# Row sums by kind, residual products spread, one convolution group earlier, in a one-core diffusion layer with 32 experts

## The chip, the cores and the metric

The kernel runs on one core of a Trainium2 chip. The metric is the device time of one execution, in microseconds (us); lower is better. Five engines work side by side, each in the order of its own queue: TensorE (PE, matrix products; its weight loads are shown as PEld), VectorE (DVE), ScalarE (ACT), GpSimd (POOL) and SyncE (SP), whose queue issues nearly all transfers from memory. They wait for one another by semaphores.

## The reference

One layer of a transformer-like block on 256 latent tokens and 256 context tokens of width 1024, in float32:

```
mod = silu(c) @ w_ada + b_ada                      # shift, scale, gate (twice)
u   = (rms_norm(x) * (1 + scale1) + shift1) @ w_in # 2560 columns, the context likewise
mix = [fourier(f) @ w_fourier, attention(q, k, v, context), b * conv3(c * h)] @ w_out
x   = x + gate1 * mix
t   = rms_norm(x) * (1 + scale2) + shift2
group = argmax(t @ w_rg); experts = top2 of (t @ w_re) in that group
y   = sum over the two experts of weight * (silu(t @ w_gate[e]) * (t @ w_up[e])) @ w_down[e]
out = rms_norm(x + gate2 * y) * norm_final
```

There are 32 experts of hidden width 512. All their weights are read, 6 MB an expert.

## The kernel before

**Weights.** All weights come through one list of transfers (`queue`, line 108), 2 MB each, that SP issues in order. Each goes into one of ten slots of 16 KB a partition (`slabs`); `take` claims a slot, `drop` gives it back when its last reader is named, and `pump` (line 123) issues the next transfers as far as slots are free. A transfer whose slot is still being read waits on SP, and all later ones wait behind it. When the prologue is over an eleventh slot is opened (`more`, line 832).

**Prologue.** The input projection, the adaLN rows, attention, the Fourier and convolution groups, the output projection and the routing logits are cut into named steps. `STEPS` (line 61) is the order in which all steps are written out by hand; each engine executes its own instructions in that order. The steps that matter here:

- `hi{n}`, `lo{n}` (lines 491 to 505): ACT rounds a piece of weights to a short form, DVE takes the rest; three buffers `ws` are used in turn, so `hi19` must wait until the products on piece 16 are done. `lo15` and `lo19` are the last readers of whole slots.
- `q0` to `q3` and `c0` to `c3` (`pairs`, line 571, through `project`, line 508): the 24 products each of one quarter of the queries and of the convolution's two factors. `q3` reads piece 15, `c0` piece 16, `c1` piece 17. `qt0` (ACT) and `qt1` (DVE) copy the finished queries.
- `ss1` (line 433, `sum_rows`, line 411): the first gate's values lie in DVE's sums over a partition each; four products with a column of ones add them over the 128 partitions, and four products with one row add the bias. Each of the four pairs writes its own 32 partitions of one PSUM bank. The other uses of `sum_rows` have no bias.
- `cs`, `csa`: four rows turned to columns by two transposes (PE), then added to a bias (DVE, line 439).
- `ch`, `w1`, `po`, `at`, `fo`, `fy`, `fz`, `mf`, `ml`: the Fourier group. `s{u}`, `X{u}`, `E{u}`, `R{u}`, `S{u}`, `t{u}`: scores (PE, line 664), row minimum (DVE, 673 and 675), exponential (ACT), scaling (DVE, ACT), transposes (PE) of the attention.

All PSUM tiles of the prologue come from one pool of eight banks (`bank`, line 255); a new tile takes a bank that an earlier reader has released.

**Routing** (lines 841 to 858). `py` holds the sums of the result in four PSUM banks; six products with the identity first put the residual `xs` there (line 846: for columns 0 to 512 two products of 512 columns, for 512 to 768 and 768 to 1024 two of 256 each). Then DVE runs the steps of `route` for both token tiles (lines 788 to 796, the last writes `msk`), five products (851 to 854, into `pr`) count the tokens ahead of each, and DVE makes the gather matrices from them (`place`, lines 821 to 823, into `fsr`).

**Experts** (line 1067). `gathered` (905) and `placed` (914, 918) fetch the up to 32 tokens of an expert, `hidden` (932) makes the 64 products with gate and up weights and drops one slot after each half, `project_down` (958) the 32 with the down weights. The next expert's gathering goes between. The sums of four experts are added to `py` by `scatter` (924) a group later, the last ones by `group_add` (1094) and `add` (1121). PSUM tiles come from a pool of seven banks (`mbank`, line 837).

Of the kernel before, what the change touches and what calls it, by code (L numbers as in the profile page):

```python
# [62 lines left out]
z1 w1 hi2 U10 H10 lo2 kx0 hi3 L10 rq1 lo3 fc1 k0 fa1 U11 U01 H11 H01 ar2 L11 hi4 L01 lo4 b3 rq2 fg1 Ba3 B3 fc2 k1 hi5 fa2 U02 lo5  # L63
U12 H02 H12 L02 L12 ar3 hi6 lo6 fg2 rq3 a0 a1 a2 fc3 k2 hi7 fa3 a3 U03 U13 lo7 H03 H13 L03 L13 a4 kv fg3 a5 a6 hi8 k3 gb ft hi9 a7
lo8 lo9 v0 hi10 a8 kt0 kt1 lo10 kt2 kt3 a9 a10 v1 a11 hi11 lo11 a12 v2 hi12 a13 lo12 a14 e0 a15 po0 hi13 e1 q0 lo13 e2 v3 hi14 e3
lo14 e4 ssh vt1 e5 hi15 q1 rsh lo15 vt0 vt3 vt2 e6 q2 hi16 e7 lo16 cs ss1 hi17 csa q3 lo17 ch0 qt1 qt0 hi18 ch1 w10 s1 lo18 w11
at0 po1 X1 s0 at1 fo0 X0 E1 fo1 s2 fy0 R1 E0 fz0 c0 c1 mf0 R0 hi19 ml0 S0 lo19 fy1 rs1 fz1 t0 S1 hi20 s3 X2 mf1 c2 z0_ y0_ E2 ml1
lo20 t1 hi21 R2 ss2 X3 z1_ S2 c3 rs2 y1_ E3 lo21 m0t00 e8 cv0 duh t2 R3 hi22 cv1 m1t00 S3 lo22 p0 cw0 m0t11 ph0 z2_ t3 y2_ cm0 pl0
m0t10 z3_ y3_ s4 cl0 cw1 m0t01 m4t11 hi23 s5 X4 cm1 m1t01 m4t00 cl1 E4 p1 X5 dg g3 R4 E5 lo23 e9 ph1 m2t00 S4 m2t11 pl1 m4t10 R5
e10 t4 S5 m4t01 g3a z4_ y4_ t5 hi24 e11 m2t10 z5_ s6 y5_ lo24 m2t01 s7 X6 hi25 m1t11 m1t10 lo25 E6 p2 X7 hi26 m5t01 ph2 m3t11 R6  # L70
# [7 lines left out]
def tile_kernel(ctx: ExitStack, tc: tile.TileContext, x, cx, small_a, small_b, b_g1, b_g2, w_ada, w_in, w_out, w_gu, w_dn, out):  # L78
    nc = tc.nc
    PE, DVE, ACT, POOL, SP = nc.tensor, nc.vector, nc.scalar, nc.gpsimd, nc.sync  # L80
# [8 lines left out]
    def blk(i, n=P):  # L89
        return slice(i * n, (i + 1) * n)  # L90
# [78 lines left out]
    cs = slab_c[:, 0:2048].rearrange("p (t f) -> p t f", t=2)  # L169
# [8 lines left out]
    bq = slab_g[:, 3332:3844]  # L178
# [14 lines left out]
    ones = keep.tile([P, P], F32, name="ones")  # L193
# [61 lines left out]
    def bank(shape=(P, 512), key=None):  # L255
        b = ps.tile(list(shape), F32, name="b", tag="b", bufs=8)
        if key is not None:
            held[key] = b
        return b
# [78 lines left out]
    def tokens(s):  # L338
        return slice(s * SEQ, (s + 1) * SEQ)
# [71 lines left out]
    def sum_rows(key, a, bias=False):  # L411

        pa = bank((P, 256), key)
        for q in range(4):
            if bias:
                r = slice(32 * (q // 2), 32 * (q // 2) + 1)
                PE.matmul(pa[blk(q, 32), :], ones[r, 0:32], bq[r, blk(q % 2, 256)], start=True, stop=False)
            PE.matmul(pa[blk(q, 32), :], ones[:, 0:32], a[:, blk(q, 256)], start=not bias, stop=True)

    def area():  # L420
# [11 lines left out]
    wr = sa[:, CA["wr"]].rearrange("p (j f) -> p j f", j=NJ)  # L432
    lb = keep.tile([P, 40], F32, name="lb")
    step["ss1"] = lambda: sum_rows("ss1", acc[:, 0:D], True)
    step["rs1"] = lambda: ACT.copy(area()["rg1"], held["ss1"])
    step["ssh"] = lambda: sum_rows("ssh", acc[:, D:2 * D])
    step["rsh"] = lambda: ACT.copy(r1, held["ssh"])
    step["cs"] = lambda: columns("cs", r1, 256)
# [370 lines left out]
    def onehot(g, st, *ts):  # L809

        for t in ts or (slice(0, 2),):
            r = rk[:, t, 4 * g:4 * g + 4]
            n = list(st[:, t].shape)
            DVE.tensor_tensor(st[:, t], r[..., None].to_broadcast(n), iota_r[:, None, :].to_broadcast(n) if len(n) == 3 else
                              iota_r[:, None, None, :].to_broadcast(n), OP.is_equal)
        return st
# [3 lines left out]
    def place(t, p):  # L820
        return [lambda: DVE.scalar_tensor_tensor(rk[:, t, :], msk[:, t, :], -OFF, p, op0=OP.mult, op1=OP.add),
                lambda: onehot(0, fsr, t),
                lambda: DVE.tensor_scalar(fsr[:, t], fsr[:, t], rr[:, t:t + 1], None, op0=OP.mult)]
# [13 lines left out]
    def mbank(shape=(P, 512), tag="b"):  # L837
        return pm.tile(list(shape), F32, name="m", tag=tag, bufs={"b": 7, "f": 1}[tag])


    py = {}
    for a, b in ((0, 512), (512, 768), (768, 1024)):
        whole = mbank((P, 2, 256)) if a else None
        for t in range(2):
            py[t, a, b] = whole[:, t, :] if a else mbank()
            PE.matmul(py[t, a, b], ident, xs[:, t, a:b], start=(t == 0 or not a), stop=False)  # L846
    pr = mbank((P, 3, NE))
    for fs in zip(*routes):
        for f in fs:
# [2 lines left out]
    for i, first_ in ((1, trib), (2, onesb)):  # L852
        PE.matmul(pr[:, i, :], onesb, msk[:, 0, :], start=True, stop=False)
        PE.matmul(pr[:, i, :], first_, msk[:, 1, :], start=False, stop=True)
    for fs in zip(place(0, pr[:, 0, :]), place(1, pr[:, 1, :])):
        for f in fs:
            f()
# [21 lines left out]
    def group(g):  # L879

        st = fst if g == 0 else onehot(g, mo.tile([P, 2, 4, CAP], F32, name="st"))
        if g:
            DVE.tensor_tensor(fsr, st, rr[:, :, None, None].to_broadcast([P, 2, 4, CAP]), OP.mult)
        state[g] = [st, None, None]

    def weighted(g):

        sw = mo.tile([P, 2, 4, CAP], F32, name="sw", tag="sw")
        POOL.tensor_tensor(sw, state[g][0], cmb[:, :, 4 * g:4 * g + 4, None].to_broadcast([P, 2, 4, CAP]), OP.mult)
        return sw  # L890

    def turned(g, sw):
        pg = mbank((P, 2, P))
        for t in range(2):
            PE.transpose(pg[:, t, :], sw[:, t], ident)
        state[g][1] = mo.tile([P, 2, P], F32, name="sl", tag="sl")
        ACT.copy(state[g][1], pg)
        return pg

    def gathered(e):  # L900

        pg = mbank((P, 256))
        for t in range(2):
            for q in range(4):
                PE.matmul(pg[32 * q:32 * q + 32, :], fsr[:, t, e % 4, :], xs[:, t, blk(q, 256)], start=(t == 0), stop=(t == 1))  # L905
        gt = mo.tile([P, 256], F32, name="gt", tag="gt")
        (DVE.tensor_copy if e == 0 else ACT.copy)(gt, pg)  # L907
        return gt

    def placed(e, gt):  # L910

        pt = mbank((P, 2, 4, CAP))
        for c in range(2):
            PE.transpose(pt[:, c], gt[:, blk(c)], ident)  # L914
        dst = xg[:, e % 4].rearrange("p (q c) n -> p c q n", c=2)
        for v, op, src in ((a2, OP.mult, pt), (sh2, OP.add, dst)):
            w = v.rearrange("p o (q c) -> p (o c) q", c=2)[..., None].to_broadcast([P, 2, 4, CAP])
            DVE.tensor_tensor(dst, src, w, op)  # L918

    def scatter(g):  # L920

        _, sl, yg = state[g]
        for (t, a, b), p in py.items():
            PE.matmul(p, sl[:, t, :], yg[:, a:b], start=False, stop=False)  # L924
# [28 lines left out]
    def project_down(e, ht, yg, i):  # L953
        wdn = loaded["dn", e].rearrange("p (q k f) -> p q k f", q=4, k=4)
        pd = mbank((P, 256))
        for k in range(4):
            for q in range(4):
                PE.matmul(pd[32 * q:32 * q + 32, :], ht[:, 32 * k:32 * k + 32], wdn[:, q, k, :], start=(k == 0), stop=(k == 3))  # L958
        drop(f"dn_{e}")
        pump()  # L960
        for q in range(4):
            rows = blk(q, 32)
            DVE.tensor_tensor(yg[blk(i, 32), blk(q, 256)], pd[rows, :], g2q[rows, :], OP.mult)  # L963

    def upto(e, also={}):

        got = {}

        def fetch():
            got["gt"] = gathered(e + 1)  # L970

        def put():
            placed(e + 1, got["gt"])

        if e in (15, NE - 1):
            return hidden(e)
        return hidden(e, {NJ: [fetch], NJ + 1: [put]} | also)

    def expert(e, also={}):
        g, i = divmod(e, 4)  # L980
        ht = upto(e, also)
        if i == 2 and g < NE // 4 - 1:
            group(g + 1)
        if i == 0:
            if g not in (0, 4):
                scatter(g - 1)
            state[g][2] = mo.tile([P, D], F32, name="yg", tag="yg")
        if i == 2:
            pg = turned(g, state[g][1])
            if e > NE - 4:  # L990

                for q in range(4):
                    (ACT.copy if q % 2 else DVE.tensor_copy)(sl1[blk(q, 32)], pg[blk(3, 32)])
        project_down(e, ht, state[g][2], i)
        if i == 1:
            state[g][1] = weighted(g)
# [69 lines left out]
    weights()  # L1066
    for e in range(NE - 4):
        expert(e)
        if e == 15:
            scatter(3)  # L1070
            n_over = nc.values_load(over[0:1, 0:1], min_val=0, max_val=1)
            with tc.If(n_over > 0):  # L1072
                overflow()
            xg = tokens()
            placed(e + 1, gathered(e + 1))
# [12 lines left out]
    e = NE - 1  # L1088
# [1 line left out]
    n = 3 * CAP  # L1090

    def group_add(k):
        (t, a, b), p = list(py.items())[k]
        PE.matmul(p, sl[0:n, t, :], yg[0:n, a:b], start=False, stop=False)  # L1094

    for k in range(6):
        group_add(k)
# [6 lines left out]
    py = {(t, a): p for (t, a, b), p in py.items()}  # L1104
# [47 lines left out]
    r = [fs[:, 6, t:t + 1] for t in range(2)]  # L1152
    a, b = 512, 768
# [95 lines left out]
```

## Time and profile before

| | us |
|---|---|
| median of 3 runs | 633.53 |
| lowest and highest | 633.09, 634.85 |
| profiled execution, whole | 633.33 |
| its span, first to last instruction | 631.5 |
| PE busy in it | 486.7 (77%) |
| DVE busy | 248.3 (39%) |
| ACT busy | 127.9 (20%) |

Times in rows are microseconds from the start of the span, unless they are marked ns. The chain of waits starts at the last instruction and goes back, at each step, to what released it; each of its pieces is a time at which nothing else would have made the end come sooner. The timeline shows instructions in order of time, neighbours of one kind merged (x8 is eight of them), with the idle time of the engine before them and who ended it in brackets. The windows give busy time of each engine in a stretch, the granted clock of TensorE (1.00 is 2.4 GHz, 0.50 is 1.2 GHz), and what the 16 DMA engines moved.

### The profile page before, as it was taken

The numbers are of one execution on the slowest core, as the hardware profiler recorded it, in microseconds if no ns is written. First come the engines' busy times: TensorE is split into PE (matmuls) and PEld (weight loads), VectorE is DVE, ScalarE is ACT, GpSimd is POOL, SyncE is SP. The second block draws the span as 40 slices with busy tenths as digits, with TensorE's granted clock in tenths as the row PEclk, the third lists the DMA queues.
The fourth block names the chain that finished last, engine by engine and source line by source line (L and its number), as shares of the span: only waits on it lengthen the run. The fifth ranks groups of instructions, "written<-read, shape, count | busy, mean of one in ns | idle before, by whom it ended". The sixth has DMA issues, their size and how long they took to land.

```text
span 631.5 us, 11826 instructions
## 1 busy us (share of the span) xinstructions
PE 486.7 (77%) x5175; PEld 301.2 (48%) x5175; DVE 248.3 (39%) x589; ACT 127.9 (20%) x281; POOL 10.1 (2%) x20
## 2 busy tenths in 40 slices
PE   3899999999989995775577666866766676568784
PEld 3788886866755553342234323433423342234442
DVE  5949784798563533111211121222132111211124
ACT  4564334765430100000000000000000000001113
POOL 1000000000000000000000000000000000000000
PEclk9899999999999999788979787888888897977998
DMA  8999983389999999999999999999999999999992
GB/s 336 425 422 404 398 342 134 134 323 393 392 398 390 428 428 427 421 428 428 424 425 428 425 425 421 423 427 429 423 425 424 427 428 425 425 425 428 425 364 92
DMA packets 21223, 246.18 MB, mean 390 GB/s; under 512 B 2214, under 2 KB 3242, under 8 KB 6956
## 3 DMA queue, kind: packets, MB, share of 16 engines
q1 hardware_dynamic: 21016, 245.08, 93.4%
q8 instruction: 43, 0.70, 0.5%
q10 hardware_dynamic: 148, 0.27, 0.1%
q14 instruction: 16, 0.13, 0.1%
HBM read 244.28 MB, written 1.05 MB: 388 GB/s over the span
## 4 chain that ended last, share of the span: by engine, by line
DMA 62%; PE 33%; DVE 2%; ACT 1%; issue 1%; DVEq 0%; SPq 0%; ACTq 0%
DMA gu<-in_w_gu 38%; DMA dn<-in_w_dn 24%; PE b L524 13%; PE b L722 4%; PE m L932 3%; PE b L664 1%; PE m L958 1%; PE b L709 1%; PE b L699 1%; PE b L310 1%; PE m L1121 1%; DVE a L293 1%; PE m L905 1%; PE m L846 1%; PE m L1094 1%
## 5 line engine op out<-in xcount | busy, mean ns | idle before, releaser
L932 PE MATMUL m<-gu,xg 128*32 128x256 f32 x2048 | 157.1, 460 | 99.3 <-DMA gu<-in_w_gu 94.3
L932 PEld LDWEIGHTS m<-gu,xg 128*32 128x32 f32 x2048 | 77.0, 127 | 172.4 <-issue 66.8
L942 DVE TENSOR_TENSOR hh<-m,sg 128x128 f32<-128x128 f32 x32 | 9.3, 292 | 221.1 <-ACT sg L940 221.1
L940 ACT ACTIVATE sg<-m 128x128 f32<-128x128 f32 x32 | 8.9, 277 | 338.1 <-PE m L932 338.1
L963 DVE TENSOR_TENSOR yg<-m,g2q 32x256 f32<-32x256 f32 x124 | 52.1, 420 | 59.0 <-PE m L958 57.7
L958 PE MATMUL m<-dn,ht 128*32 128x256 f32 x992 | 61.1, 387 | 8.7 <-DMA dn<-in_w_dn 7.4
L524 PE MATMUL b<-uh,ws 128*128 128x256 f32 (+1 forms) x240 | 52.3, 309 | 0.0
L958 PEld LDWEIGHTS m<-dn,ht 128*32 128x32 f32 x992 | 31.1, 110 | 30.0 <-issue 7.6
L524 PEld LDWEIGHTS b<-uh,ws 128*128 128x128 f32 x240 | 39.5, 190 | 4.8 <-issue 2.8
L905 PE MATMUL m<-xs,fsr 128*32 128x256 f32 x512 | 38.6, 420 | 3.2 <-PEq L1072 2.2
L524 PE MATMUL b<-ul,ws 128*128 128x256 f32 (+1 forms) x120 | 36.3, 306 | 0.0
L524 PE MATMUL b<-ws,uh 128*128 128x512 f32 (+1 forms) x96 | 26.5, 364 | 2.4 <-ACT uh L353 2.4
L500 DVE TENSOR_TENSOR ws<-in,ws 128x1024 fp32r<-128x1024 f32 x20 | 24.4, 1223 | 9.3 <-ACT ws L495 9.2
L905 PEld LDWEIGHTS m<-xs,fsr 128*32 128x32 f32 x512 | 19.0, 125 | 18.7 <-issue 9.7
L924 PE MATMUL m<-yg,sl 128*128 128x256 f32 (+1 forms) x84 | 27.1, 473 | 1.0 <-DVE yg L963 1.0
L495 ACT CAST ws<-in 128x1024 fp32r<-128x1024 f32 x20 | 21.0, 1048 | 32.4 <-PE b L524 30.7
L722 PE MATMUL b<-ws,cat 128*128 128x512 f32 x96 | 27.4, 414 | 0.0
L524 PEld LDWEIGHTS b<-ul,ws 128*128 128x128 f32 x120 | 22.9, 193 | 0.9
L918 DVE TENSOR_TENSOR xg<-m,a 128x256 f32<-128x256 f32 x32 | 13.6, 425 | 21.9 <-PE m L914 21.9
L914 PE MATMUL m<-ident,gt 128*128 128x128 f32 x64 | 14.0, 301 | 9.3 <-ACT gt L907 8.2
L924 PEld LDWEIGHTS m<-yg,sl 128*128 128x128 f32 x84 | 16.1, 198 | 10.7 <-issue 7.8
L722 PEld LDWEIGHTS b<-ws,cat 128*128 128x128 f32 x96 | 16.5, 188 | 7.5 <-issue 4.1
(250 smaller groups left out, 497.6 us busy)
## 6 DMA issues: line engine op xcount, KB each, us to landing
gu<-in_w_gu SPq DMA_DIRECT2D x63, 2048.0 KB, 39.3
dn<-in_w_dn SPq DMA_DIRECT2D x31, 2048.0 KB, 39.2
ada<-in_w_ada SPq DMA_DIRECT2D x12, 2048.0 KB, 12.5
in<-in_w_in SPq DMA_DIRECT2D x3, 2048.0 KB, 9.5
in<-in_w_in SPq DMA_DIRECT2D x8, 512.0 KB, 15.9
out<-in_w_out SPq DMA_DIRECT2D x2, 2048.0 KB, 8.9
gu<-in_w_gu SPq DMA_DIRECT2D x4, 512.0 KB, 28.5
dn<-in_w_dn SPq DMA_DIRECT2D x3, 512.0 KB, 11.5
```

The lines of the kernel that those rows point to most:

```text
L495: ACT.copy(ws[:, 0], loaded[kind, i][:, blk(c, 1024)])
L500: DVE.tensor_tensor(split[n][:, 1], loaded[kind, i][:, blk(c, 1024)], split[n][:, 0].bitcast(F32), OP.subtract)
L524: PE.matmul(po, st, mv, start=begins, stop=(c == 3 and tail and not any(po is v[1] for v in todo[n + 1:])))
L722: PE.matmul(held["yo", t, h], held["cat"][:, a, MIX[n], blk(t)], ws[:, b, h, :], start=(held["nm", t, h] == 0), stop=(held["nm", t, h] == ...
L905: PE.matmul(pg[32 * q:32 * q + 32, :], fsr[:, t, e % 4, :], xs[:, t, blk(q, 256)], start=(t == 0), stop=(t == 1))
L914: PE.transpose(pt[:, c], gt[:, blk(c)], ident)
L918: DVE.tensor_tensor(dst, src, w, op)
L924: PE.matmul(p, sl[:, t, :], yg[:, a:b], start=False, stop=False)
L932: PE.matmul(pg[32 * q:32 * q + 32], xg[:, e % 4, j, :], wgu[j // 4][:, :, j % 4, q * P:(q + 1) * P], start=(j == 0), stop=(j == NJ - 1))
L942: DVE.tensor_tensor(hh, pg[:, 1, :], sg, OP.mult)
L958: PE.matmul(pd[32 * q:32 * q + 32, :], ht[:, 32 * k:32 * k + 32], wdn[:, q, k, :], start=(k == 0), stop=(k == 3))
L963: DVE.tensor_tensor(yg[blk(i, 32), blk(q, 256)], pd[rows, :], g2q[rows, :], OP.mult)
```

## The change

In `sum_rows` the four bias products come first, then the four sums; before they alternated. In `STEPS`, `q3` moves ahead of `cs` and `ss1`, and `c0` moves from before `c1` to after `ch1`, ahead of `s1`. Of the six residual products the two of columns 768 to 1024 stay ahead of the routing, the two of 512 to 768 go behind the five counting products, and the two of 0 to 512 go behind expert 1. `group_add` sorts the pieces so that it takes them in the order it had; `scatter` now takes them in the new order.

```diff
-lo14 e4 ssh vt1 e5 hi15 q1 rsh lo15 vt0 vt3 vt2 e6 q2 hi16 e7 lo16 cs ss1 hi17 csa q3 lo17 ch0 qt1 qt0 hi18 ch1 w10 s1 lo18 w11
-at0 po1 X1 s0 at1 fo0 X0 E1 fo1 s2 fy0 R1 E0 fz0 c0 c1 mf0 R0 hi19 ml0 S0 lo19 fy1 rs1 fz1 t0 S1 hi20 s3 X2 mf1 c2 z0_ y0_ E2 ml1
+lo14 e4 ssh vt1 e5 hi15 q1 rsh lo15 vt0 vt3 vt2 e6 q2 hi16 e7 lo16 q3 cs ss1 hi17 csa lo17 ch0 qt1 qt0 hi18 ch1 c0 w10 s1 lo18 w11
+at0 po1 X1 s0 at1 fo0 X0 E1 fo1 s2 fy0 R1 E0 fz0 c1 mf0 R0 hi19 ml0 S0 lo19 fy1 rs1 fz1 t0 S1 hi20 s3 X2 mf1 c2 z0_ y0_ E2 ml1
...
         pa = bank((P, 256), key)
+        for q in range(4) if bias else ():
+            r = slice(32 * (q // 2), 32 * (q // 2) + 1)
+            PE.matmul(pa[blk(q, 32), :], ones[r, 0:32], bq[r, blk(q % 2, 256)], start=True, stop=False)
         for q in range(4):
-            if bias:
-                r = slice(32 * (q // 2), 32 * (q // 2) + 1)
-                PE.matmul(pa[blk(q, 32), :], ones[r, 0:32], bq[r, blk(q % 2, 256)], start=True, stop=False)
             PE.matmul(pa[blk(q, 32), :], ones[:, 0:32], a[:, blk(q, 256)], start=not bias, stop=True)
...
-    for a, b in ((0, 512), (512, 768), (768, 1024)):
+
+    def residual(a, b):
         whole = mbank((P, 2, 256)) if a else None
         for t in range(2):
             py[t, a, b] = whole[:, t, :] if a else mbank()
             PE.matmul(py[t, a, b], ident, xs[:, t, a:b], start=(t == 0 or not a), stop=False)
+
+    residual(768, 1024)
     pr = mbank((P, 3, NE))
...
+    residual(512, 768)
     for fs in zip(place(0, pr[:, 0, :]), place(1, pr[:, 1, :])):
...
         expert(e)
+        if e == 1:
+            residual(0, 512)
...
-        (t, a, b), p = list(py.items())[k]
+        (t, a, b), p = sorted(py.items(), key=lambda v: (v[0][1], v[0][0]))[k]
```

## Rows read from the trace of the kernel before

**Rows 1.** The page: data rate in 40 slices of 15.8 us each.

```profile
GB/s 336 425 422 404 398 342 134 134 323 393 392 398 390 428 428 427 421 428 428 424 425 428 425 425 421 423 427 429 423 425 424 427 428 425 425 425 428 425 364 92
```

**Rows 2.** The chain of waits in order of time: start, length, engine and line.

```profile
90.46 0.57 PE b L418 x8
...
97.10 0.54 PE b L417 x2
...
100.92 0.55 PE b L418 x2
101.47 3.02 PE b L524 x24
104.49 1.73 PE b L596 x8
106.22 1.06 PE b L664 x4
...
180.93 3.71 PE m L846 x12
...
188.84 5.35 PE m L932 x64
...
197.83 3.45 PE m L932 x64
...
214.17 32.15 DMA dn<-in_w_dn
```

**Rows 3.** Windows: a stretch, then each engine's busy time, TensorE's clock, DMA share, GB/s.

```profile
130.00:165.00 35.00, 35.00 (x232) 22.46 (x233) 28.23 (x70) 20.47 (x39) 0.00 (x0) 1.00 0.99 401
...
192.00:195.00 3.00, 3.00 (x53) 1.87 (x45) 0.29 (x1) 0.28 (x1) 0.00 (x0) 0.93 0.82 246
```

**Rows 4.** SP's waits between 98 and 119 and between 182 and 193; its timeline there.

```profile
SPq L152 <- DVE ws L500: 21.3, 1, 21.3
...
SPq L152 <- PE m L932: 11.3, 1, 11.3
...
117.84 10.13 SPq L152 DMA_DIRECT2D ada<-in_w_ada  x2
...
192.39 0.33 SPq L152 DMA_DIRECT2D dn<-in_w_dn  x1
```

**Rows 5.** Timeline: four products of one row each, in one run.

```profile
187.75 0.63 PE L1063 MATMUL m<-sa,ones 1*32 1x256 f32 x8
```

**Rows 6.** Timeline of DVE and ACT between 84 and 122.

```profile
103.13 0.17 DVE L439 TENSOR_TENSOR sh<-b,sa 128x8 f32<-128x8 f32 x1 [6.61 <-DMA sa<-in_b_g]
...
104.53 0.69 DVE L580 COPY a<-b 128x512 f32<-128x512 f32 x1
...
107.31 0.42 DVE L673 CUSTOM_DVE_ANT_0 acc<-b,a 128x256 f32<-128x256 f32 x1 [0.48 <-PE b L664]
...
109.43 0.42 DVE L673 CUSTOM_DVE_ANT_0 acc<-b,a 128x256 f32<-128x256 f32 x1 [0.29 <-PE b L664]
...
116.58 1.23 DVE L500 TENSOR_TENSOR ws<-in,ws 128x1024 fp32r<-128x1024 f32 x1 [2.21 <-ACT ws L495]
...
115.50 1.05 ACT L495 CAST ws<-in 128x1024 fp32r<-128x1024 f32 x1 [1.89 <-PE b L524]
```

**Rows 7.** Timeline of the routing.

```profile
182.52 0.31 DVE L796 TENSOR_TENSOR msk<-oh 128x32 bf16<-128x32 f32 x2
...
184.47 0.18 PE L851 MATMUL m<-msk,trib 128*128 128x32 bf16 x1
...
184.79 0.28 DVE L821 SCALAR_TENSOR_TENSOR rk<-msk,m 128x32 f32<-128x32 bf16 x2 [1.96 <-PE m L854]
...
185.76 1.07 PE L905 MATMUL m<-xs,fsr 128*32 128x256 f32 x16 [1.00 <-DVE fsr L823]
```

**Rows 8.** Windows over the first expert's products.

```profile
189.50:192.00 2.50, 2.50 (x28) 1.62 (x24) 0.79 (x4) 0.00 (x0) 0.61 (x1) 0.50 1.01 433
...
192.50:193.00 0.50, 0.50 (x16) 0.38 (x12) 0.00 (x0) 0.00 (x0) 0.00 (x0) 1.00 0.74 295
```

## The prediction

> **What bounds the kernel now.** I read the page's data rate first. From the 14th slice on it stands at 421 to 429 GB/s, almost to the end, while the two slices around 95 to 126 us have 134 [rows 1]: so the time is a long stretch in which the transfers never rest, put behind a prologue in which they do. Second, the chain of waits: up to 181 us it is nearly all PE, piece after piece, through the routing and the first experts PE and DVE, and from 214.17 on only transfers that queue behind one another [rows 2]. Third, the windows: PE is busy 35.00 of 35 us in the prologue's second half, DVE 28.23 [rows 3]. Fourth, SP's waits: its longest one, 21.3 us, is for DVE's last reading of a slot (`lo19`), and the last long one, 11.3 us, for the first half of expert 0's products, after which it issues at 192.39 [rows 4]. Around that moment the rate falls to 246 GB/s over 3 us [rows 3]; against 426 that is 540 KB short, or 1.27 us of transfer time. It is the last hole. After it an expert takes PE about 7.2 us (two from 197.83 to 214.17, less half an expert's 3.45 [rows 2]) and gives back three slots, whose filling takes 3 x 4.9 us (2.1 MB at 426 GB/s). PE is then always ahead.
>
> So what counts is when the transfers become unbroken. Two things set that: when the last transfers issued during the prologue run dry (call it D), and when expert 0 gives back its first slot (R, at 192.39). If everything up to 181 comes earlier by p, D moves by p. If the routing gives another r, R moves by p + r. The end moves by p plus the part of the hole that closes, at most 1.27 us.
>
> **Part 1, the row sums.** Today eight products alternate, bias, sum, bias, sum: from 97.10 to 101.47, eight pieces of 0.54 or 0.55, 4.37 us in all [rows 2]. The same four sums without bias take 0.57 when they run together, as at 90.46 [rows 2], since the four write different quarters of the partitions. Four one-row products in one run take 0.63 [rows 5], the nearest row to the bias group. That makes 0.57 + 0.63 = 1.2 us, with 0.1 for the one change between the kinds 1.3; 4.37 - 1.3 = 3.1 us less PE, on the path. The bounds: at best no change of kind costs anything (-3.2); at worst the four bias products don't overlap, four at 0.54 as now, so 2.16 + 0.57 = 2.73 and -1.6. I take 3.1, since [rows 5] is the same form.
>
> One difference speaks against it: the products at 187.75 read four different groups of rows, while the bias products share two, two by two. The Trainium skill (TensorE: Matmul & The Clock Gate, Part 3: Packing small matmuls) says that a weight load overlaps running products only where the row group differs; by that two and two would follow each other. The four sums share all rows and run in 0.57 together [rows 2], so the row says otherwise; by the page the gain would be nearer the 1.6, which is a rival below.
>
> **Part 2, q3 and c0 moved.** Nothing is added: 24 products each, 3.02 us [rows 2], change place on an engine that never idles there. So PE gains nothing by itself, and the question is who now waits. From about 97 PE does q3 (3.02), the columns, the sums (1.3), ch0 and ch1 (1.73), c0 (3.02) and s1 (1.06): s1 ends near 107.2, where it ends now, at 107.28 [rows 2], so the first row minimum still starts near 107.3 [rows 6]. The saved 3.1 us stand in PE's queue as c0 already done. DVE is held till 103.13 by a transfer that doesn't move [rows 6], and after it has the copy `qt1` and two `lo` steps to do; with c0 ahead of s1 PE has work meanwhile. Between 107.3 and 118 DVE must make up 3.1 us. It can: its largest pause there, 2.21 us, is for the cast `hi19`, which waited for c0's products on PE (ACT idle 1.89) [rows 6], and c0 is now long done; smaller pauses add the rest. I expect `lo19`, and with it the transfer that heads SP's queue, 2.5 us before 117.84, between 0 and 3.1; behind it stand the last adaLN and the first expert weights, whose users also come 3 us earlier. I put the lag that reaches PE at 0, bounds 0 to 2.9. So p = 3.1.
>
> **Part 3, the residual products.** Six products of 2048 columns take 3.71 us [rows 2], 0.46 for 256 columns. DVE has `msk` ready at 182.83 (182.52 + 0.31), but the counting products start at 184.47, behind the residual, and DVE goes on at 184.79 after 1.96 us of waiting for them [rows 7]. With only two residual products in front (0.93), PE is free at 181.86, and the count can start at 182.85; it takes 0.32 as now, so DVE goes on at 183.2: r = 1.6. The bounds are 0 and the whole pause, 1.96. The next two products (0.93) follow the count, from 183.2 to 184.1, under DVE's 0.97 (184.79 to 185.76); the gather then starts at 184.2 rather than 185.76. If DVE were faster they would cost up to 0.93. The last two, 1.85 us, lie behind expert 1. PE issues nothing late by that but slots of expert 2; by then the six slots of experts 0 and 1 stand in SP's queue, 6 x 4.9 = 29 us of transfers against 7.2 + 1.85 us of PE. Cost nothing; without that cover 1.85. The new order in `scatter` lets its first product wait for DVE's last piece; also covered by the transfers.
>
> **The sum.** R moves by 3.1 + 1.6 = 4.7, D by 3.1, and the hole's 1.27 us closes whole, as R needs to gain only 1.27 on D. The end moves by 3.1 + 1.27 = 4.4 us; 0.3 of r is left over. The profiled execution took 633.33 (span 631.5, 1.8 around it), 0.2 below the median of 633.53: 628.9 by the one, 629.1 by the other. I give 629.1.
>
> **Rivals.**
>
> (a) The clock falls earlier. Today it is at 0.50 from about 189 to 192.4, which is why expert 0's products take 5.35 rather than 3.45 us: 1.9 us [rows 2, 8]. PE loses 1.85 us of residual work out of the stretch before it and pauses twice more. If the fall comes while the gather (1.07), the transposes and the one-row products (0.63) run, those double and cost with the transposes about 2, while the expert's slow part shrinks or stays. Then R moves by 2.7 to 3.1, nothing of the hole closes, and the end is 633.5 - 3 = 630.6. For it: PE already pauses there, 1.00 us ahead of the gather [rows 7], and the clock fell after that. Against: the routing gets shorter by about as much (1.6) as it loses. The Trainium skill (TensorE: Matmul & The Clock Gate, Part 1) tells that the half rate is the default and that activity lifts it, which speaks against taking products out of the routing.
>
> (b) DVE doesn't make up the 3.1 us. It is held to 103.13 by a transfer, the first row minimum moves by 0.2 at most, and later DVE is busy 28.23 of 35 [rows 3, 6]. If PE then waits for scaled rows, p is 0.2 to 1.8, and the end 633.5 - p - 1.27: 630.4 to 632.0, and I put it at the upper end.
>
> (c) The bias products don't overlap, so the change doesn't do what it says: p = 1.6, 633.5 - 1.6 - 1.27 = 630.6.
>
> (d) Slower, by banks. c0's two sums now occupy two of eight PSUM banks from 103 on. If c0's second bank is the one that `qt1` frees, at 105.22 [rows 6], c0 starts 2.2 us late; and if s0 and s2 then each wait for the bank of a row-minimum pair (2.1 us from 107.31 to 109.43 [rows 6]), PE loses 2.2 + 4.2 = 6.4 us. From a loss of 4.4 on the change is a loss; this gives 633.5 + 2.0 = 635.5. Against: `qt0` frees a bank right after q3, long before c0.
>
> **How the numbers follow.** The forecast has 0.62, its own range 628.2 to 630.0; (a) 0.13, (b) 0.14, (c) 0.07, (d) 0.04. A measurement of this kernel can tell 0.3%, or 1.9 us, from no change: below 631.6 counts as faster, above 635.4 as slower. The forecast, (a), (c) and nearly a third of (b) are faster: 0.85; the rest of (b) and half of (d) the same: 0.12; slower 0.03. The range takes in (a), (c) and (b) up to 632.0 and, below, 1 us for a hole larger than I count: 628.0 to 632.0. It leaves out (d) and the tails.
>
> **What the profile after would show.** Eight L417 instructions in one run of about 0.6 us and L418 behind them in 0.57; `lo19` and its transfer near 115.3; the logits' end near 177.5 rather than 180.6; L846 in three places; the pause before L821 near 0.4 instead of 1.96; SP's issue for expert 0's first half near 187.7; no window as low as 246 GB/s after it. The prediction is wrong if PE shows waits for DVE between 107 and 175, if the sums still take over 2 us, if the clock is at 0.50 over the gather, or if the rate of 426 is broken later than now.

## The result, and the profile after

The kernel after took 629.75 us (median of 5 runs, 629.53 to 631.94) against 633.53 for the kernel before: a ratio of 0.9937, 95% interval 0.9919 to 0.9955, or 4.0 us less with 2.9 to 5.1. The forecast was 629.1. Its profiled execution took 629.93 (span 628.1). A later series of the same kernel, told below, gave 0.9945. Medians and ratios here are those of undisturbed runs: one run each of v3 and v4 and two of v5 below, 697 to 1130 us long, are slow ones and stay out.

The first view is the page's data rate, to be read beside [rows 1]: the slow stretch (slices 7 and 8) is still there, and the slice behind it, the ninth, has risen from 323 to 385.

```profile
GB/s 352 425 421 393 398 352 136 151 385 392 390 403 420 426 424 427 429 423 428 423 426 429 424 428 422 424 427 423 429 429 422 426 426 425 430 424 428 422 342 80
```

Part 1, in PE's timeline (start, length, engine, line, operation, tiles, shape, count): the eight products stand in two runs, the bias first, and the last row tells where PE goes on.

```profile
99.62 0.63 PE L416 MATMUL b<-g,ones 1*32 1x256 f32 x8
100.19 0.64 PE L418 MATMUL b<-acc,ones 128*32 128x256 f32 x8
100.75 1.99 PE L596 MATMUL b<-f 128*128 128x256 f32 x8
```

From 99.62 to 100.75 that is 1.13 us, where the pieces from 97.10 on took 4.37 [rows 2]: p = 3.24. The bias run costs 0.57, no more than the sums' own run of 0.56, although its products share groups of rows two by two. The view of the weight loads (PEld) tells the two orders apart. In the kernel before the loads stood idle for 0.41 us ahead of each bias and each sum but the first. Now the four products of one form have all their loads within 0.15, while the products run; the idle 0.41 is left only where the form changes. The first two lines are of the kernel before, the third is of the kernel after:

```profile
99.21 0.13 PEld L417 LDWEIGHTS b<-g,ones 1*32 1x32 f32 x2 [0.41 <-issue]
99.75 0.14 PEld L418 LDWEIGHTS b<-acc,ones 128*32 128x32 f32 x2 [0.41 <-issue]
```

```profile
99.62 0.15 PEld L416 LDWEIGHTS b<-g,ones 1*32 1x32 f32 x8 [0.17 <-PE b L524]
```

A rival would be that each sum waited for the bias below it, in the same quarter of PSUM. But the pieces from a sum to the next bias, which share no quarter, cost the same 0.54 or 0.55 [rows 2].

Part 2, in DVE's timeline (the bracket: idle time and what ended it), SP's waits and SP's issues. DVE is held by the same transfer until 103.64, 0.5 later than in [rows 6], the first row minimum starts 0.65 us earlier, and SP's transfer behind `lo19` goes out at 115.20, 2.64 before that of [rows 4]. The wait of PE for DVE that the prediction feared isn't there: between 98 and 177 the view of PE's own waits has one row, of 0.2 us.

```profile
103.64 0.17 DVE L439 TENSOR_TENSOR sh<-b,sa 128x8 f32<-128x8 f32 x1 [6.38 <-DMA sa<-in_b_g]
...
106.66 0.42 DVE L673 CUSTOM_DVE_ANT_0 acc<-b,a 128x256 f32<-128x256 f32 x1
```

```profile
115.20 0.33 SPq L152 DMA_DIRECT2D ada<-in_w_ada  x1
...
186.38 0.33 SPq L152 DMA_DIRECT2D dn<-in_w_dn  x1
```

Part 3, PE's and DVE's timeline of the routing, beside [rows 7]. DVE now waits 0.34 for the counts where it waited 1.96, r = 1.62. Expert 0's 64 products take 3.66 (5.35 before [rows 2]), and its first slot is issued again at 186.38 (above), 6.01 us earlier than in [rows 4].

```profile
177.46 1.83 PE L847 MATMUL m<-xs,ident 128*128 128x256 f32 x4 [0.35 <-DVE lg L788]
179.29 0.18 PE L854 MATMUL m<-msk,trib 128*128 128x32 bf16 x1
...
179.50 1.92 PE L847 MATMUL m<-xs,ident 128*128 128x256 f32 x4
181.35 1.07 PE L909 MATMUL m<-xs,fsr 128*32 128x256 f32 x16
...
184.39 3.66 PE L936 MATMUL m<-gu,xg 128*32 128x256 f32 x64 [0.41 <-DVE xg L922]
```

```profile
179.05 0.31 DVE L796 TENSOR_TENSOR msk<-oh 128x32 bf16<-128x32 f32 x2
179.70 0.29 DVE L821 SCALAR_TENSOR_TENSOR rk<-msk,m 128x32 f32<-128x32 bf16 x2 [0.34 <-PE m L857]
...
180.33 0.48 DVE L823 TENSOR_SCALAR fsr<-fsr,cst 128x128 f32<-128x128 f32 x2
```

The residual's four-instruction groups take 1.83 and 1.92 where 0.93 was counted. The windows tell why (a stretch, its length, busy time of PE, PEld, DVE, ACT and POOL, TensorE's granted clock, DMA share, GB/s): the clock is at 0.50, the lower of its two levels, over the routing, and back at 1.00 before expert 0; before, it was low over expert 0 [rows 8]. What PE did ahead of the fall: it worked without a gap to 177.1, paused 0.35 for DVE and began the residual. And behind the first slot's issue the rate stays at 344 and more, its lowest at 189 to 190, where before it had gone to 246 over 3 us [rows 3].

```profile
177.00:178.00 1.00, 0.65 (x3) 0.50 (x3) 0.86 (x9) 0.00 (x0) 0.00 (x0) 0.87 0.97 377
178.00:179.00 1.00, 1.00 (x4) 0.63 (x3) 1.00 (x11) 0.00 (x0) 0.00 (x0) 0.50 0.93 393
...
181.00:182.00 1.00, 1.00 (x14) 0.42 (x16) 0.10 (x2) 0.98 (x6) 0.00 (x0) 0.92 1.05 434
...
189.00:190.00 1.00, 0.77 (x7) 0.36 (x10) 0.41 (x2) 0.35 (x1) 0.00 (x0) 1.00 0.83 344
190.00:191.00 1.00, 1.00 (x24) 0.64 (x20) 0.73 (x2) 0.00 (x0) 0.00 (x0) 1.00 0.94 393
```

The end, in the chain of waits (start, length, what): the last transfer of the chain lands at 599.72, then a chain of some 28 us of PE, DVE and ACT follows. In the chain of before (first line) the same transfer was issued at 563.86 and took 39.26. Here (the other lines) the issue is 4.52 us earlier, the landing 3.40.

```profile
563.86 39.26 DMA dn<-in_w_dn
```

```profile
559.34 40.38 DMA dn<-in_w_dn
...
599.86 1.97 PE m L962 x32
```

**A table for the experiments.** From the trace's records of the transfers in the kernel's main queue I counted when 64 MB (the prologue's end) and 200 MB (deep in the long stretch) had arrived, against the one trace of before, which has them at 188.7 and 510.8. The last columns have the issue of expert 0's returned first slot, and the span against that of before, 631.5.

| kernel | at 64 MB | at 200 MB | first slot | span |
|---|---|---|---|---|
| before | 0 | 0 | 192.39 | 0 |
| after | -3.7 | -4.8 | 186.38 | -3.4 |
| v1_sums_back | +0.7 | -0.6 | 189.17 | +0.4 |
| v2_order_back | -3.5 | -4.7 | 186.88 | -4.2 |
| v3_residual_back | -4.3 | -4.2 | 187.02 | -3.4 |
| v5_residual_only | -0.5 | -1.7 | 189.07 | -0.8 |
| v6_first_slot_late | -3.7 | -2.0 | 190.58 | -1.7 |
| v7_residual_later | -2.7 | -3.2 | 188.65 | -2.4 |
| v9_sums_only | -3.3 | -2.9 | 188.45 | -1.6 |
| v12_after_again | -3.3 | -3.0 | 189.35 | -0.1 |
| v11_gain_only | -3.8 | -5.1 | 185.76 | -3.4 |
| v4_tail | -3.6 | -4.6 | 186.49 | -4.3 |
| v8_tail_gain | -3.7 | -5.0 | 185.97 | -5.3 |
| v10_tail_on_before | -0.9 | -0.5 | 191.90 | -1.7 |

The step between the first two columns is what the hole gained or lost. v10, which is the kernel before up to its tail, shows how far two executions differ by themselves: 0.5 to 0.9.

The table also tells when the hole closes. Count from the moment of the 64 MB to the first slot's issue: where that is 1.7 us or less (after, v1, v2, v4, v5, v8, v11), the step gains 1.0 to 1.4; at 2.6 (v3, v7) it gains nothing in v3 and 0.5 in v7; from 3.0 to 4.1 (before, v9, v10, v12) the hole stays or grows by up to 0.4; at 5.6 (v6) it grows by 1.7.

The experiments were run in series of their own, in which the kernel before took 633.6 to 634.2 in the median. So their ratios are compared, not their medians; "scaled" below is a ratio times 633.53, to be held against the expected times.

### The profile page after: what moved, and what is told of

The parts are those of the page before. It is cut to its first block, busy times and chain, and to the rows that moved or that the text cites. A ratio compares the mean times of both kernels' runs of the same rounds, so it can differ in the third digit from the quotient of the medians.

```text
span 628.1 us, 11826 instructions
## 1 busy us (share of the span) xinstructions
PE 485.4 (77%) x5175; PEld 300.5 (48%) x5175; DVE 247.9 (39%) x589; ACT 127.8 (20%) x281; POOL 10.1 (2%) x20
```

## The experiments

**The parts taken back one by one.** v1 has the change, but bias and sum alternate again.

```diff
-        for q in range(4) if bias else ():
-            r = slice(32 * (q // 2), 32 * (q // 2) + 1)
-            PE.matmul(pa[blk(q, 32), :], ones[r, 0:32], bq[r, blk(q % 2, 256)], start=True, stop=False)
         for q in range(4):
+            if bias:
+                r = slice(32 * (q // 2), 32 * (q // 2) + 1)
+                PE.matmul(pa[blk(q, 32), :], ones[r, 0:32], bq[r, blk(q % 2, 256)], start=True, stop=False)
```

> The changed kernel with the eight bias and sum products of the first gate alternating again; the other two parts stay. Theory A (the transfers become unbroken earlier by the prologue's gain plus the hole of 1.27 us): without the 3.24 us of the sums (4.37 before, 1.13 measured after) only the hole's closing is left, so the transfers run about 1.2 us ahead of the kernel before and the end lies 0.9 to 1.3 us under it, near 632.4. Rival B (the routing's own gain is worth more than the hole, up to the 6.0 us by which expert 0's first slot came back earlier, less 3.2): 630.7.

633.52, ratio 0.9991 (0.9976 to 1.0006), scaled 633.0: no gain is left that stands clear of the noise. PE's eight pieces are back at 0.54 or 0.55 each, the 64 MB arrive no earlier than before, and the hole closes by 1.3. By the interval the end moved between 1.5 earlier and 0.4 later, so the runs don't exclude the expected 632.4; Rival B's 630.7 they do.

v2 has the change, but the old order list, with q3 and c0 where they were.

```diff
-... e7 lo16 q3 cs ss1 hi17 csa lo17 ch0 qt1 qt0 hi18 ch1 c0 w10 s1 ...
-... fy0 R1 E0 fz0 c1 ...
+... e7 lo16 cs ss1 hi17 csa q3 lo17 ch0 qt1 qt0 hi18 ch1 w10 s1 ...
+... fy0 R1 E0 fz0 c0 c1 ...
```

> The changed kernel with q3 and c0 at their old places in the hand-written order; sums and residual stay changed. Theory A (PE is never idle there, so the order alone is worth nothing): 629.8, within 0.4 of the changed kernel, transfers ahead by 4.5 or more. Rival C (the order is what lets the sums' gain through, since VectorE is held to about 103 us by the gate rows' transfer while s1 would come 3 us earlier): part of the 3.24 us is lost again after 103 us, end at 630.8 to 632, and PE shows waits for VectorE or ScalarE between 100 and 130 us.

629.91, ratio 0.9944 (0.9928 to 0.9960), beside 0.9937 with the new order. PE has no wait for DVE before the logits but one of 0.2, as after: the order list is worth nothing at the end that these runs can tell. But the transfer behind `lo19` goes out earlier without the moves, 3.97 us ahead of before instead of 2.64:

```profile
113.87 10.13 SPq L152 DMA_DIRECT2D ada<-in_w_ada  x2
```

With the moves and the grouped sums it goes out at 114.6 to 115.6 in eight profiles, without the moves at 113.9 (v2, v9). So they hold this transfer back by about a microsecond, which doesn't reach the logits.

v3 has the change, but all six residual products in front of the count.

```diff
+    residual(0, 512)
+    residual(512, 768)
     residual(768, 1024)
...
-    residual(512, 768)
...
-        if e == 1:
-            residual(0, 512)
```

> The changed kernel with all six residual products ahead of the routing again; sums and order stay changed. Theory A: the prologue's 3.4 us stay, nothing of the hole closes, transfers ahead by 3.4 to 3.5 instead of 4.7; the window around the return of expert 0's first slot falls to some 250 GB/s again. End 1.2 us above the changed kernel if the end follows the transfers (631.0). Rival D (the last landings or PE at the end set the time, since the changed kernel gave back 1 us there): 629.8 to 630.2.

630.29, ratio 0.9948 (0.9931 to 0.9966), scaled 630.2. DVE waits 1.96 for the counts again, and the hole stays, as its windows show: 69% of the transfer engines' time in two us in a row.

```profile
188.00:189.00 1.00, 1.00 (x28) 0.71 (x20) 0.00 (x0) 0.24 (x1) 0.00 (x0) 1.00 0.69 246
189.00:190.00 1.00, 0.82 (x13) 0.22 (x5) 0.43 (x2) 0.40 (x2) 0.00 (x0) 1.00 0.69 197
```

By the ratios that is 0.7 above after, where 1.2 was expected, and the intervals overlap. Here the clock wasn't low at all between 160 and 200 and expert 0's products took 3.66; the first slot went out at 187.02, and still the hole stayed.

**The parts alone.** v9 is the kernel before with part 1 only, v5 with part 3 only (the same lines as above, put into the kernel before).

> The kernel before with its row sums grouped by kind, and nothing else: order list and residual products stay as they were. Theory A (the sums carry nearly the whole gain and the order list nothing): the logits end 3.2 us earlier, the transfers run 3 to 4 us ahead of the kernel before, the hole after expert 0's first slot stays, and the end comes 3.0 us earlier, as where the residual products alone were put back: 630.5. Theory B (the grouped sums need q3 and c0 moved to reach the logits): waits of PE for DVE after the first row minimum, the logits only 1 to 2 us earlier, 631.5 to 632.5. Theory C (nothing is given back in the tail without the residual part): the end gains all that the transfers gain, 629.9.

> The kernel before with the residual products spread as in the changed kernel, and nothing else: sums alternate, q3 and c0 stand at their old places. Theory A (closing the hole is worth its 1.27 us): transfers ahead by 1.2, end 0.9 to 1.3 under the kernel before, 632.4. Theory G (the residual part is worth its hole only where nothing later gives it back; the run with the sums alternating showed the transfers 0.6 ahead and an end like before): 633.0 to 633.6. If the run with the moved order lost time by that order, this one is clearly under it (by 0.8).

v9: ratio 0.9959 (0.9946 to 0.9973), 2.6 us less (1.7 to 3.4), scaled 630.9 where 630.5 was expected; the transfers run 3.3 ahead up to the prologue's end, and the hole takes 0.4 back. PE waits for DVE at most 0.2 us before the logits, so the sums need no help from the order list. v5: ratio 0.9990 (0.9978 to 1.0002); the first slot goes out 3.32 us earlier and the hole closes, a step of 1.2 between the columns. In its windows the rate holds where [rows 3] has 246:

```profile
192.00:193.00 1.00, 0.90 (x14) 0.57 (x18) 0.62 (x2) 0.04 (x1) 0.00 (x0) 1.00 1.04 426
193.00:194.00 1.00, 1.00 (x25) 0.57 (x20) 0.43 (x1) 0.00 (x0) 0.00 (x0) 1.00 1.00 426
```

Alone its gain at the end, 0.6 by the ratio, lies between 0 and 1.4; that doesn't decide between Theory A and Theory G.

**The hole tested from the other side.** v6 has the change, and six idle products of 256 columns, no part of the computation, ahead of expert 0.

```diff
+    for _ in range(6):
+        PE.matmul(mbank((P, 256), "f"), ident, xs[:, 0, 0:256], start=True, stop=True)
```

> The changed kernel with six idle products of 256 columns (2.6 us) ahead of expert 0's products, so that its first slot comes back near 189.0 instead of 186.4. Theory A (the end moves by what the transfers lose, and they run dry near 189.9, so the slot has to come back 2 to 4 us before): the hole opens again, by 0.9 to 1.3 us, transfers ahead by 3.4 to 3.8 and the end near 630.8. Rival H (PE is on the path there): the whole 2.6 us, 632.3. Rival I (the transfers aren't sensitive to it): 629.8.

631.38, ratio 0.9955 (0.9938 to 0.9972), scaled 630.7, beside the expected 630.8. The idle products take 4.38 us at the full clock, where the residual's price of 0.46 for 256 columns gives 2.8, and the gather ahead of them ran at the lower clock (1.94 instead of 1.07); the first slot goes out at 190.58, still 1.8 ahead of before. Yet the hole is 1.7 wider than before's, since the transfers run dry 3.7 us earlier. So the hole is set by the one moment less the other, as the prediction has it:

```profile
189.00:190.00 1.00, 1.00 (x25) 0.61 (x20) 0.00 (x0) 0.09 (x1) 0.00 (x0) 1.00 0.41 164
190.00:191.00 1.00, 1.00 (x27) 0.57 (x23) 0.00 (x0) 0.00 (x0) 0.00 (x0) 1.00 0.08 33
```

**A try to do better at the routing.** v7 puts the residual products of columns 512 to 768 behind expert 1 too, to free the gather from them.

```diff
-    residual(512, 768)
...
         if e == 1:
+            residual(512, 768)
             residual(0, 512)
```

> The changed kernel with the two residual products of columns 512 to 768 also behind expert 1. In the changed kernel they ran at the lower clock, 1.92 us, and the gather started after them at 181.35 where its matrices were ready at 180.8. Theory A: gather and first slot come 0.4 to 0.6 us earlier, the hole is closed already, so the end stays at 629.8, within 0.4. Rival: the routing is on the path, 629.3.

630.79, ratio 0.9951 (0.9934 to 0.9969), scaled 630.4 where 629.8, within 0.4, was expected; the intervals of v7 and after overlap, so the times don't tell them apart. In its profile the clock stays low till 188.4; the gather and expert 0's products run at half rate, and the first slot is 2.3 us later than after:

```profile
180.86 1.93 PE L908 MATMUL m<-xs,fsr 128*32 128x256 f32 x16 [1.01 <-DVE fsr L823]
...
185.00 5.30 PE L935 MATMUL m<-gu,xg 128*32 128x256 f32 x64
```

I first took that for the price of PE's pause of 1.01, but the next run forbids to call it shown.

**The kernel after once more.** Its first profile gained 4.8 us in the transfers and 3.4 in the span; the same kernel was profiled again to see whether that belongs to the change.

> The kernel after once more, profiled a second time, to see whether its tail gives back what the transfers gain. Theory A (the late landing belongs to the change): expert 0's first slot at 186 to 187, the transfers ahead of the kernel before by 4.6 us, the last down projection slot of expert 30 landing 40.4 us after its issue again and only 3.4 us ahead of the kernel before, the median at 629.8. Theory B (it was the spread of one execution): the landing 39.2 us after the issue, as in the kernel before, 4.5 us ahead of it, the profiled run at 628.7 to 629.0, and the ratio of the medians nearer to 0.9928 than to 0.9937.

630.77, ratio 0.9945 (0.9927 to 0.9963), scaled 630.0. The late landing doesn't belong to the change: the same transfer took 39.18 this time, which speaks against Theory A. But neither theory had seen what came. The same instructions, with the same 0.35 us of PE's pause ahead of the residual, got another clock: low for 10.2 us, from 178.6 to 188.8, over gather and expert 0, where in the first profile it was low for 3.4, from 177.7 to 181.2.

```profile
177.80 1.35 PE L847 MATMUL m<-xs,ident 128*128 128x256 f32 x4 [0.35 <-DVE lg L788]
179.84 2.06 PE L847 MATMUL m<-xs,ident 128*128 128x256 f32 x4
181.82 1.94 PE L909 MATMUL m<-xs,fsr 128*32 128x256 f32 x16
185.97 5.04 PE L936 MATMUL m<-gu,xg 128*32 128x256 f32 x64
```

```profile
188.00:189.00 1.00, 1.00 (x16) 0.50 (x12) 0.00 (x0) 0.00 (x0) 0.37 (x1) 0.59 1.03 442
189.00:190.00 1.00, 1.00 (x28) 0.52 (x24) 0.00 (x0) 0.00 (x0) 0.00 (x0) 1.00 0.45 180
190.00:191.00 1.00, 1.00 (x24) 0.57 (x20) 0.00 (x0) 0.00 (x0) 0.00 (x0) 1.00 1.24 279
191.00:192.00 1.00, 1.00 (x20) 0.38 (x9) 0.29 (x1) 0.33 (x2) 0.00 (x0) 1.00 0.56 180
```

The first slot went out at 189.35, 3.04 earlier than before, the hole stayed open (180, 279, 180 GB/s), and this execution took 633.23: of the 3.0 us that its transfers were ahead, the last landing kept 0.1.

```profile
325.43 39.16 DMA dn<-in_w_dn
...
364.66 40.69 DMA gu<-in_w_gu
...
563.85 39.18 DMA dn<-in_w_dn
...
603.17 1.97 PE m L962 x32
```

The chain of before has these transfers too:

```profile
325.42 39.26 DMA dn<-in_w_dn
...
364.75 40.20 DMA gu<-in_w_gu
```

So the 3.0 us weren't lost at the last landing. From 325 on the chain, in which each issue follows the landing before it, runs at the times of before, although the bytes stay some 3 us ahead to 240 MB. Behind the first link, all take from 39.1 to 40.7 us, here and in the other traces (the last one of v8 apart); what the end follows is where the chain starts and what these links add up to, and not the mean progress of the bytes.

Of the eleven timed runs of the kernel after seven lie from 629.42 to 630.14, four from 631.40 to 633.23. That the clock parts them isn't shown: it was seen in one of the four only, and the kernel before spreads as far, from 632.64 to 636.13 in one series.

How often the clock falls this way the other profiles tell, since after, v2, v4, v8, v11 and v12 execute the same routing. In all six it falls between 176.5 and 178.6. Over the gather it is still low in two (v2 and v12, 1.94 each), over expert 0 in v12 alone. The first slot goes out between 185.8 and 186.9 in five, and at 189.35 in v12.

**The tail.** In after's first profile the clock is low once more, over expert 30's first half, where PE had waited 4.07 for weights, and I took that for the place of the lost microsecond. v4 puts four sums of the last group into the places of four idle products in expert 31, so that only two stand in the chain ahead of it; v8 also moves the gain rows from inside expert 30 ahead of it; v11 does that last step alone; v10 does v8's two steps in the kernel before. (The idle products, which v4, v8 and v10 leave out, are no part of the computation.)

```diff
-    expert(NE - 2, {3: [gain_rows]})
+    gain_rows()
+    expert(NE - 2)
...
-    for k in range(6):
+    for k in range(2):
         group_add(k)
...
-    ht = hidden(e, {4: [warm], 5: [warm], 6: [warm], NJ: [warm]})
+    ht = hidden(e, {j: [partial(group_add, k)] for j, k in ((4, 2), (5, 3), (6, 4), (NJ, 5))})
```

> The changed kernel with four of the last six group sums moved in between the last expert's products, in the place of the four idle products that stood there to keep TensorE busy (these are left out). Theory E (behind the landing of expert 30's last weights the time is a chain of PE work, so the transfers' lead has little to do with its length): 1.8 us less PE in that chain, end at 628.0. Rival F (the last expert's weights land too late for that, pieces of its gate and down weights are waited for): 629.3 to 629.8, with PE waits for transfers behind 604 us.

> The kernel with the reordered group sums at the end, and the 16 products that spread the last norm's gains (2.0 us) moved from the middle of expert 30 to ahead of it, into the 4 us in which PE waits for expert 30's weights. Theory E (from the landing of expert 30's first weights PE is the chain, slowed by the lower clock that the wait before leaves behind): 2.0 us less behind that landing, and less time at the lower clock; the landing of expert 30's last weights becomes the later one, so 1 to 1.5 us under the 628.9 of the kernel with the reordered sums: 627.5. Rival F (landings decide): 628.9.

> The kernel after with the gain rows put ahead of expert 30, and the six group sums and the idle products as they were. Theory A (the two edits of the tail are worth 0.9 each and add): 628.9. Theory B (only together with the group sums moved): 629.6 to 629.8. In either case expert 0's first slot and the transfers' lead (4.6 us) should stand as in the kernel after.

> The kernel before with the two edits of the tail alone (four group sums in place of the four idle products of expert 31, which are no part of the computation; gain rows ahead of expert 30). Theory A (after the change the tail gives 1 us back because expert 30's second half falls on the half clock there, and the edits repair that): the kernel before has that half at 1.93 us, so only what the edits save in PE's last chain is gained here, 0 to 0.9: 632.7 to 633.5. Theory B (the edits shorten the chain of the tail wherever it stands): 1.7 us as behind the change, 631.8.

| kernel | median | ratio | interval | scaled |
|---|---|---|---|---|
| v4_tail | 628.75 | 0.9918 | 0.9897 to 0.9938 | 628.3 |
| v8_tail_gain | 628.01 | 0.9910 | 0.9891 to 0.9928 | 627.8 |
| v11_gain_only | 630.10 | 0.9928 | 0.9908 to 0.9947 | 629.0 |
| v10_tail_on_before | 633.15 | 0.9981 | 0.9968 to 0.9995 | 632.3 |

The profile of v11 refutes the low clock as the cause of the microsecond that after's first profile lost. Its two halves of expert 30 run at 1.93 each, and the down projection still starts at 599.86, as after, because the transfer lands no earlier:

```profile
590.04 1.93 PE L936 MATMUL m<-gu,xg 128*32 128x256 f32 x32 [0.31 <-DMA gu<-in_w_gu]
594.85 1.93 PE L936 MATMUL m<-gu,xg 128*32 128x256 f32 x32 [2.88 <-DMA gu<-in_w_gu]
...
599.86 1.93 PE L962 MATMUL m<-dn,ht 128*32 128x256 f32 x32 [1.01 <-DMA dn<-in_w_dn]
```

The times don't decide between its theories: both 628.9 and 629.8 lie within the interval. Nor is the low clock harmless in every execution: the chains of v2, v4, v7 and v9 end on an earlier transfer and go through expert 30's first half, and there that half takes 2.43 to 3.56 instead of the 1.86 of the second:

```profile
590.77 3.55 PE m L936 x32
...
596.33 1.86 PE m L936 x32
```

(These are v4's.) v10 shows what the sums do: they shorten the chain behind the last landing wherever it stands. In its chain the group sums ahead of expert 31 take 1.96 where after's, like before's, takes 3.68.

```profile
606.22 1.96 PE m L1095 x4
```

1.7 us less in the chain; measured 1.2 (0.3 to 2.0) on before, between the expectations of Theory A and Theory B, and by the ratios 1.2 (v4) and, with the gain rows moved too, 1.7 (v8) behind the change. v4 and v8 come near their Theory E (628.0 and 627.5), though Rival F (629.3 and 628.9) still lies within their intervals. v8 has the lowest ratio of all; its interval and after's overlap.

## Why the prediction was right, and where it wasn't

- **Part 1**, 3.1 us: 3.24 in the rows, and the kernel without it (v1) loses the gain while the kernel with it alone (v9) keeps 2.6. The rival that the bias products don't overlap fell. The Trainium skill (TensorE: Matmul & The Clock Gate, Part 3: Packing small matmuls) says that a weight load overlaps running products only where the row group differs; the trace disagrees here, since four products on two groups of rows had their loads within 0.15 us and took 0.57.
- **Part 2**, nothing, with `lo19`'s transfer 2.5 earlier: 2.64 after. For the end it is nothing, as v2 and v9 show; the transfer is helped by the sums and held back by the moves (3.97 without them). DVE made up what the sums saved, so the rival on DVE fell; so did the banks, as PE has no such wait.
- **Part 3**, r = 1.6: 1.62. That the pair of products behind the count costs nothing was wrong where the clock is low: 1.92 instead of 0.93, so that the gather starts at 181.35, 0.5 after DVE's last step for it has ended (180.33 + 0.48).
- **The first slot**, p + r = 4.7 earlier: 6.0 in one execution, 3.0 in the other. The step that failed is that expert 0's 5.35 us would stay as it was. It isn't a property of the kernel: v10, the kernel before up to there, had the low clock from 180.5 to 183.9 and expert 0 in 3.66; v1, v3 and v5 had none at all between 160 and 200. Rival (a) had this, with the first slot 2.7 to 3.1 earlier and the hole open; it is what the second profile shows (3.04), and by the prediction's own sign, the clock at 0.50 over the gather, that execution counts against it. One of six profiles with this routing shows rival (a) whole, so the runs don't tell that its 0.13 was wrong.
- **The hole**, 1.27 us: it closes by 1.1 in after's first profile and by 1.2 in v5, and stays in v3 and v12. The step "R needs to gain only 1.27 on D" was too small. Before, the slot went out 3.7 us after the 64 MB; v3 gained 1.1 on that and v7 1.0, and they closed nothing and 0.5; from a gain of 2.0 on (v2) it closes whole. The forecast's 1.6 lies between. With the predicted slot at 187.7 and the 64 MB at 185.0 of after's first profile, 2.7 us apart, most of the hole would have stayed. That it closed is luck as far as the prediction goes: the clock fell earlier and left expert 0 the full clock, at 3.66. In the ratios the part comes to between nothing and 1.4 us (v5).
- **The sum**, 4.4: the transfers of the first profile gained 4.8 against one trace of before, the medians 3.8. Two things stand between. Some executions keep the hole. And in all nine traces whose tail wasn't edited the span gains less than the transfers, by 0.4 to 2.9 us, the middle 0.9, even in v1, whose time can't be told from that of the kernel before. The end follows a chain of landings with links of 39.1 to 40.7 us, and not the mean progress of the bytes: after's last link took 40.38 where that of before took 39.26, and v12's chain ran as late as before's with its bytes 3.0 ahead. The step "the end moves by what the transfers gain" is thus too large by about 1 us as measured against the one trace of before. The landings spread by themselves, in before too (39.16 to 40.20); whether that trace was a lucky one in its tail, and what decides where the longer links fall, stays open. The forecast of 629.1 came within 0.7 of 629.75 with two terms that were right (p and r), one that luck saved (the hole) and a last step, from the transfers to the end, that was too large.

## What to carry to other kernels

Small products of two forms that alternated on PE took 0.54 us each here; given in two runs by form, eight took 1.13 us instead of 4.37, and that was most of the gain (2.6 of 4.0 us by itself, v9). Where a long stretch is bound by transfers, look for the last moment at which they run dry: work counts there only by the difference of two moments, and the slack that it is given has to cover the clock's worst place, not the place that one profile shows. And ahead of the end, follow the chain of landings itself, and count what stands behind the last one: there 1.7 us of products less gave 1.2 (v10).

## What the runs showed that I had not expected

- The granted clock of one and the same kernel was low for 3.4 us (177.7 to 181.2) in one execution and for 10.2 us (178.6 to 188.8) in another, with the same pause of 0.35 us ahead of it. The first slots of the two lie 3.0 us apart, 0.3 of which was there before the routing, the 200 MB 1.8, the times 3.3; the rest of the 3.3 arose in the chain of landings. The runs don't show what decides the clock.
- The same 64 products of expert 0 took 3.66, 5.04, 5.30 or 5.35 us, as the clock fell.
- The transfer of expert 30 that the end hangs on took 39.2 to 39.6 us from issue to landing in eight profiles, and 40.38 in after's. That is nothing special: links of 40.1 to 40.7 stand at other places of the same chains in the other profiles, so that each transfer's landing, and not the rate, says when the end comes.
